# A two-part network on one core: first norms summed on TensorE, rotary tables moved, the FFN's scale deferred

## The chip, the cores and the metric

The kernel runs on one core of a Trainium2 chip. The metric is the device time of one execution in microseconds: the median of 3 runs is 1226.24 us (1225.2 to 1228.88). The profiled execution took 1224.34 us, with a span of 1222.2 us between its first and last instruction.

## The reference

Everything is fp32, for 256 positions of 1024 channels. The first block has two layers of a pooling mixer with dilated attention, a squared-ReLU FFN, and a gated per-layer embedding. The second block is one layer with modulated norms, a gated delta rule in both directions over a context and the latent, a short convolution, a Fourier branch, gates over the three, and a SwiGLU.

```
hn = rmsnorm(h, norm1[i]);  z = hn @ w_in[i]          # u, q, k, v;  q, k get rotary on 16 of 64 dims
h = h + concat([pool(u), attention(q, k, v)]) @ w_out[i]
hn = rmsnorm(h, norm2[i])
h = h + square(relu(hn @ w_up[i])) @ w_down[i]
h = h + sigmoid(rmsnorm(h, norm3[i]) @ w_gate[i]) * (p[i] @ w_ple[i])
...
mod = silu(c) @ w_mod + b_mod;  h = modulate(x, norm1_g, sh1, sc1);  hc = modulate(ctx, ...)
o_ctx, o_lat = bidir_gated_delta(context, latent)      # chunks of 64, a triangular inverse per chunk
x = x + g1 * (gates_0 * y_dn + gates_1 * y_sc + gates_2 * y_fn) @ w_o
x = x + g2 * swiglu(modulate(x, norm2_g, sh2, sc2))
return rmsnorm(x, final_g)
```

A row's scale commutes with both the ReLU (it is positive) and the matrix product over channels: with a row factor r, `square(relu(r·y)) @ w = r² · (square(relu(y)) @ w)`.

## The kernel before

Activations lie feature by position: `h` is 128 partitions by 8 blocks of 256 positions. Weights come in units of 512 KB by DMA into `wst` (three buffers, issued on SyncE's queue). ScalarE rounds a half of a unit to its high part `wh` (L262), VectorE takes the remainder `wl` (L263), and each product is three matmuls, hi·hi, lo·hi and hi·lo (`mm3`, L274). Operands are split the same way into `xh` and `xl` (L297, L298; L911, L912 for modulated norms). PSUM has four `acc` and four `bank` tiles. A norm's gain goes into the split; its row factor is applied to the product. For that `sumsq` squares `h` by two blocks (L309), adds the squares as `ssp` (L317, L319, L323), `col_sums` adds over partitions by a matmul with ones, `root` finds the inverse root by nine small operations on VectorE (`rsv`, `rsy`, `rst`, L345 to L361), and `across` turns it into a row (L370) where one is wanted.

`proj` does the first projection by four quarters of 256 channels; its norm's squares are added on GpSimd. `ffn` runs 16 steps of two `up` units and, one step behind, two `down` units into the four `acc`; the products of the first steps wait for the row of roots and are then scaled and rectified in one (L716). `residual` (L704) adds the accumulators to `h`. `gate` follows it directly.

Side work runs as generators: `beside(gen, rate)` attaches one, and `tick` in the matmul helpers advances it `rate` steps per unit. Such are the `modulation` (48 loads of `w_mod`, 512 KB each, and products with `c` on VectorE, L882; parts in three groups, beside the first FFN, later, and in the mixer), `context` (the context's half of the delta rule, between the layers' attention and beside the second FFN) and the recurrence in the mixer. There the triangular inverses are built by blocks: GpSimd and three DMAs (`there`, `back`, `xc`, L1275 to L1301) make the base blocks, and `dn_merge` joins them on TensorE (`U,al`; `U` and `Tm` on VectorE, L1317). `self.trip` says after how many steps the joining follows the round trip. `dn_scan` makes four steps for the latent: `S,kT`, then VectorE's `dr` (L1374, L1375), `dr,W`, `dv`, `S,qg`. A scheduler lists each engine's instructions in one order; at run time each engine works its list front to back. `np1` and `np2` count halves of weights whose `wl` goes to GpSimd.

Of the kernel before, what the change touches and what calls it, by code (L numbers as in the profile page):

```python
# [230 lines left out]
class Net:  # L231
# [218 lines left out]
    def rotary(self):  # L450
# [42 lines left out]
    def proj(self, i, b, x, r):  # L493

        nc = self.nc
        z = self.b1.tile([P, 2, 512], F32, name="zv" if b > 2 else "zqk")
# [4 lines left out]
        first = r is None
        if first:
            if i == 0:
                self.setup2()
            r = self.norm_cols(self.h)
        for t in range(2):
            nc.scalar.activation(z[:, t], pt[t], AF.Copy, scale=r[:, t:t + 1])
        return (z, r) if first else z

    def rotate(self, z):  # L510
        nc = self.nc
        zz = z.rearrange("p t (h d) -> p t h d", d=HD)
        x1, x2 = zz[:, :, :, 0:8], zz[:, :, :, 8:16]
        co = self.cos[:, :, None, :].to_broadcast([P, 2, 8, 8])
        si = self.sin[:, :, None, :].to_broadcast([P, 2, 8, 8])
        w = [self.b1.tile([P, 2, 8, 8], F32, name=f"rot{j}", bufs=1) for j in range(4)]
# [182 lines left out]
    def residual(self, acc):  # L699
        h = self.h  # L700
        for j in range(4):
            for n in ((0, 1), (1, 2)) if j == 3 else ((0, 2),):
                js = slice(2 * j + n[0], 2 * j + n[1])
                self.nc.vector.tensor_add(h[:, js], h[:, js], acc[j][:, n[0]:n[1]])  # L704

    def ffn(self, i):
# [17 lines left out]
        r = []  # L724
        steps = self.row_steps_sb(self.h, r)
        next(steps)
        wait = []
        for f in range(16):
            bv = self.bank2()
            if f == 0 and self.ko & 4:  # L730
                self.cols_into(bv, [self.a["w_up"][i, n] for n in range(2)], x, True)
            for n in range(2):
                if f or not self.ko & 4:
                    self.cols_into(bv[:, n:n + 1], [self.a["w_up"][i, 2 * f + n]], x)
                if f == self.at[0] and n == self.at[1]:
                    next(steps)
                if f == self.at[2] and n == self.at[3]:
                    run(steps)
                    for b in wait:
                        square(b)  # L740
                    wait = None
            if wait is not None:
                wait.append(bv)
            else:
                square(bv)
                while len(pend) > 1:
                    down(False)
        self.residual(down(True))
# [171 lines left out]
    def context(self, d, e):  # L920
# [17 lines left out]
        yield from self.modulate(Halves(hc), self.gains[:, 1], self.mod[:, 0, 1], x)  # L938
# [836 lines left out]
    def run(self):  # L1775
# [5 lines left out]
        self.np1 = 3  # L1781
        self.np2 = 3
# [17 lines left out]
        self.rp = 0  # L1800
# [13 lines left out]
        self.trip = 10  # L1814
        self.mod_parts = (((1, 0, 2), (3,), (4, 5)), ((1, 0, 2), (), (3, 4, 5)), ((1, 0, 2, 3), (), (4, 5)), ((1, 0), (), (2, 3, 4, 5)))[1]
# [47 lines left out]
```

## Time and profile before

| | |
|---|---|
| median of 3 runs | 1226.24 us (1225.2 to 1228.88) |
| profiled execution, span | 1224.34 us, 1222.2 us |
| granted TensorE clock, mean | 0.986 |
| TensorE (PE) busy | 1174.3 us (96%) |
| VectorE (DVE) busy | 899.3 us (74%) |
| ScalarE (ACT) busy | 635.6 us (52%) |
| GpSimd (POOL) busy | 119.9 us (10%) |
| DMA | 221.43 MB, 181 GB/s |

In the rows below, "idle 5.35 <-DVE U L1317" in square brackets is how long the engine stood before an instruction and what released it. A granted clock of 1.00 is 2.4 GHz throughout, 0.50 would be 1.2 GHz throughout. A row of several instructions (xN) gives the time from the first's start to the last's end. An fp32 matmul of few columns appears as two rows.

### The profile page before, as it was taken

How to read it: one execution, taken by the hardware profiler on the slowest of the kernel's cores; microseconds unless marked ns; L12 is line 12 of the kernel's file. 1: busy time of each engine (PE TensorE's matmuls, PEld its weight loads, DVE VectorE, ACT ScalarE, POOL GpSimd, SP SyncE). 2: the span in 40 equal slices, each digit the busy share in tenths (PEclk: the TensorE clock that was granted, in tenths of full speed). 3: DMA queues.
4: the chain of work that ended last, by engine and by line, in shares of the span. 5: the costliest groups of instructions: out<-in, count | busy, mean ns of one | idle time of the engine just before them, and what ended most of it. 6: DMA issues, size and time to landing. Idle time of an engine off the chain costs nothing.

```text
span 1222.2 us, 24807 instructions
## 1 busy us (share of the span) xinstructions
PE 1174.3 (96%) x9882; PEld 1111.4 (91%) x9882; DVE 899.3 (74%) x1804; ACT 635.6 (52%) x1250; POOL 119.9 (10%) x207
## 2 busy tenths in 40 slices
PE   8999899999999989999999999997999999999997
PEld 6779899999977889999999979897989998999996
DVE  6998997556998488675657899897655768555555
ACT  5654645545755565644445555544333546544444
POOL 1000000000010000064000130275000000000000
PEclk9999999999999999999999989999999998999998
DMA  6767688555553645556444525677422452655552
GB/s 223 238 199 249 208 297 278 189 194 190 164 174 121 200 139 164 182 165 207 156 147 164 171 91 164 226 270 243 142 89 100 173 195 99 213 185 189 186 180 84
DMA packets 65779, 221.43 MB, mean 181 GB/s; under 512 B 10048, under 2 KB 11456, under 8 KB 65664
## 3 DMA queue, kind: packets, MB, share of 16 engines
q1 hardware_dynamic: 64800, 218.29, 53.4%
q0 software_dynamic: 864, 1.57, 0.6%
q8 instruction: 77, 1.26, 0.4%
q14 instruction: 38, 0.31, 0.1%
HBM read 218.00 MB, written 1.84 MB: 180 GB/s over the span
## 4 chain that ended last, share of the span: by engine, by line
PE 72%; DVE 13%; DMA 6%; POOL 4%; issue 3%; ACT 2%; SPq 0%; DVEq 0%; POOLq 0%; ACTq 0%
PE acc L274 38%; PE bank L274 33%; DVE wl L263 4%; DMA wmst<-w_mod 2%; DVE xl L298 1%; POOL bo L1288 1%; POOL bz L1289 1%; ACT wh L262 1%; DVE wmst L882 1%; PE bank L565 1%; DVE h L704 1%; DVE cy L1044 1%; DMA back<-bzt 1%; DVE qkT L533 1%; DMA pt<-pT 0%
## 5 line engine op out<-in xcount | busy, mean ns | idle before, releaser
L262 ACT ACTIVATE wh<-wst 128x512 fp32r<-128x512 f32 x708 | 411.9, 624 | 427.4 <-PE bank L274 157.3
L263 DVE TENSOR_TENSOR wl<-wst,wh 128x512 fp32r<-128x512 f32 x702 | 470.1, 703 | 208.5 <-ACT wh L262 208.0
L274 PE MATMUL bank<-xl,wh 128*128 128x256 f32 x992 | 280.5, 283 | 2.1 <-DVE xl L298 2.1
L274 PE MATMUL bank<-xh,wl 128*128 128x256 f32 x992 | 279.4, 282 | 2.9 <-DVE wl L263 2.9
L274 PE MATMUL bank<-xh,wh 128*128 128x256 f32 x992 | 281.3, 284 | 0.8 <-ACT wh L262 0.8
L274 PE MATMUL acc<-al,wh 128*128 128x256 f32 x688 | 191.6, 279 | 0.0
L274 PE MATMUL acc<-ah,wl 128*128 128x256 f32 x688 | 191.3, 279 | 0.0
L274 PE MATMUL acc<-ah,wh 128*128 128x256 f32 x688 | 191.2, 279 | 0.0
L274 PEld LDWEIGHTS bank<-xh,wl 128*128 128x128 f32 x992 | 187.0, 189 | 4.3 <-DVE wl L263 4.3
L274 PEld LDWEIGHTS bank<-xl,wh 128*128 128x128 f32 x992 | 187.0, 189 | 2.8 <-DVE xl L298 2.7
L274 PEld LDWEIGHTS bank<-xh,wh 128*128 128x128 f32 x992 | 187.1, 189 | 1.6 <-ACT wh L262 1.2
L274 PE MATMUL acc<-xh,wh 128*128 128x256 f32 x640 | 183.4, 287 | 2.2 <-ACT xh L911 2.2
L274 PE MATMUL acc<-xl,wh 128*128 128x256 f32 x640 | 182.0, 285 | 1.5 <-DVE xl L912 1.5
L274 PE MATMUL acc<-xh,wl 128*128 128x256 f32 x640 | 181.1, 284 | 0.5 <-DVE wl L263 0.4
L274 PEld LDWEIGHTS acc<-al,wh 128*128 128x128 f32 x688 | 129.0, 188 | 0.0
L274 PEld LDWEIGHTS acc<-ah,wl 128*128 128x128 f32 x688 | 128.9, 188 | 0.1
L274 PEld LDWEIGHTS acc<-ah,wh 128*128 128x128 f32 x688 | 128.9, 188 | 0.0
L274 PEld LDWEIGHTS acc<-xh,wh 128*128 128x128 f32 x640 | 121.6, 190 | 4.7 <-ACT xh L911 2.8
L274 PEld LDWEIGHTS acc<-xl,wh 128*128 128x128 f32 x640 | 121.5, 190 | 2.9 <-DVE xl L912 1.7
L274 PEld LDWEIGHTS acc<-xh,wl 128*128 128x128 f32 x640 | 121.9, 191 | 1.5 <-DVE wl L263 0.9
L274 PE MATMUL acc<-wl,xh 128*128 128x512 f32 x176 | 70.6, 401 | 2.5 <-DVE wl L263 2.4
L274 PE MATMUL acc<-wh,xh 128*128 128x512 f32 x176 | 70.8, 406 | 1.1 <-ACT wh L262 1.1
(365 smaller groups left out, 1564.8 us busy)
## 6 DMA issues: line engine op xcount, KB each, us to landing
wst<-w_up SPq DMA_DIRECT2D x64, 512.0 KB, 4.2
wst<-w_down SPq DMA_DIRECT2D x64, 512.0 KB, 4.2
wmst<-w_mod SPq DMA_DIRECT2D x48, 512.0 KB, 4.8
wst<-w_fin SPq DMA_DIRECT2D x44, 512.0 KB, 3.2
wst<-w_in SPq DMA_DIRECT2D x39, 512.0 KB, 3.6
wst<-w_mgate SPq DMA_DIRECT2D x24, 512.0 KB, 3.3
wst<-w_fout SPq DMA_DIRECT2D x22, 512.0 KB, 3.2
wst<-w_qkv SPq DMA_DIRECT2D x20, 512.0 KB, 3.4
```

Source lines behind the costliest of these rows:

```text
L262: nc.scalar.activation(wh[:, c:c + n], st[:, c:c + n], AF.Copy)
L263: i = (nc.gpsimd if self.onpool > 0 else nc.vector).tensor_tensor(wl[:, c:c + n], st[:, c:c + n], wh[:, c:c + n].bitcast(F32), op=OP.subtract)
L274: self.nc.tensor.matmul(out, lhsT, rhs, start=start, stop=stop, skip_group_check=skip)
L298: nc.vector.scalar_tensor_tensor(xl[:, k], src, gain, xh[:, k].bitcast(F32), op0=OP.mult, op1=OP.subtract)
L533: nc.vector.tensor_copy(qk[:, :, t * P:(t + 1) * P], bk.rearrange("p (c q) -> p c q", c=4))
L565: nc.tensor.transpose(bk[:, c * P:(c + 1) * P], s[:, g, c * P:(c + 1) * P], self.ident)
L704: self.nc.vector.tensor_add(h[:, js], h[:, js], acc[j][:, n[0]:n[1]])
L882: nc.vector.scalar_tensor_tensor(pr, st, 1.0, cv[v], op0=OP.mult, op1=OP.mult, accum_out=mod[:, part, v, k:k + 1])
L1044: nc.vector.scalar_tensor_tensor(y4[:, j], pad[:, j, :, tap:tap + CHUNK], w[:, j, tap:tap + 1], y4[:, j], op0=OP.mult, op1=OP.add)
L1288: pool.tensor_tensor(o, lt[:, c:, j:c].to_broadcast([P, n, c]), Z[:, j:c, 0:c].to_broadcast([P, n, c]), op=OP.mult)
L1289: pool.tensor_tensor(Z[:, c:, 0:c], Z[:, c:, 0:c], o, op=OP.subtract)
```

## The change

1. The first norm of each layer is summed by quarters. Behind each quarter of the first projection, two blocks of `h` are squared on ScalarE and summed over partitions by four matmuls with ones into one bank. `norm_cols` and GpSimd's adds go.
2. The rotary tables (`rp` 0 to 1) and their two loads are made behind the second projection, not in `setup`. They are expanded to all heads, and a rotation takes three operations on 128x256 in place of twelve on 128x64.
3. The FFN no longer waits for its row of roots: ReLU on ScalarE, squares as before, and `residual` multiplies each accumulator by the row of 1 / mean square (`mean_square_steps`, no root) before adding it.
4. `mod_parts` puts 32 of the 48 `w_mod` units beside the first FFN (24 before), 16 later, none in the mixer (24 before); the first rate is 0.55 for 0.85.
5. `np1`, `np2`: six halves of `wl` go from GpSimd to VectorE. `trip` 10 becomes 13, and the context's norm gives way four times more.

```
-            r = self.norm_cols(self.h)
+            if first:
+                sq = self.t2k("sq")
+                nc.scalar.activation(sq, self.h[:, 2 * q:2 * q + 2], AF.Square)
+                for n in range(2):
+                    for t in range(2):
+                        self.mm(cs[:, t:t + 1], sq[:, n, t * P:(t + 1) * P], self.ones[:, 0:1], q == 0 and n == 0 and t == 0,
+                                q == 3 and n == 1, True)
...
+            r = self.rsqrt(cs, 2, D)
...
-        for o, x, c in zip(w, (x1, x2, x2, x1), (co, si, co, si)):
-            for t in range(2):
-                nc.vector.tensor_mul(o[:, t], x[:, t], c[:, t])
-        for t in range(2):
-            nc.vector.tensor_sub(x1[:, t], w[0][:, t], w[1][:, t])
-            nc.vector.tensor_add(x2[:, t], w[2][:, t], w[3][:, t])
+        nc.vector.tensor_mul(co, zz, self.cos)
+        nc.vector.tensor_mul(si, zz[:, :, ::-1], self.sin)
+        nc.vector.tensor_add(zz, co, si)
...
-                self.nc.vector.tensor_add(h[:, js], h[:, js], acc[j][:, n[0]:n[1]])
+                a = acc[j][:, n[0]:n[1]]
+                if row is not None:
+                    t = self.t2k("fft")[:, n[0]:n[1]]
+                    self.nc.vector.tensor_mul(t, a, row[:, None, :].to_broadcast([P, n[1] - n[0], T]))
+                    a = t
+                self.nc.vector.tensor_add(h[:, js], h[:, js], a)
+
+    def mean_square_steps(self, h, res):
+        ss = self.sumsq(h)
+        yield
+        v = self.sm.tile([P, 2], F32, name="rsv2")
+        nc.vector.tensor_scalar(v, self.col_sums((ss,)), 1.0 / D, EPS, op0=OP.mult, op1=OP.add)
+        nc.vector.reciprocal(v, v)
+        yield
+        r = self.sm.tile([P, T], F32, name="nrow")
+        nc.scalar.activation(r, self.across(v)[:, 0:T], AF.Copy)
+        res.append(r)
...
-                nc.vector.scalar_tensor_tensor(t[:, n], bv[:, n], 0.0, r[0], op0=OP.max, op1=OP.mult)
+            if f in (1, 3, 5):
+                next(steps, None)
+            nc.scalar.activation(t, bv, AF.Relu)
...
-        self.residual(down(True))
+        self.residual(down(True), r[0])
...
-            self.beside(self.modulation(*self.mod_parts[0]), 0.85)
+            self.beside(self.modulation(*self.mod_parts[0]), 0.55)
...
+        for _ in range(4):
+            yield
...
-        self.np1 = 3
-        self.np2 = 3
+        self.np1 = 0
+        self.np2 = 0
...
-        self.trip = 10
+        self.trip = 13
```

Three places of the lists, as the scheduler orders them. First VectorE at the end of the first FFN, where `acc` holds the `down` products and `xl` is the gate's operand; before:

```order
L263 TENSOR_TENSOR wl<-wst,wh 128x512 x4
L704 TENSOR_TENSOR h<-h,acc 128x512 x2
L298 SCALAR_TENSOR_TENSOR xl<-h,k_norm_242,xh 128x256 x2
L704 TENSOR_TENSOR h<-h,acc 128x512
L298 SCALAR_TENSOR_TENSOR xl<-h,k_norm_242,xh 128x256 x2
L704 TENSOR_TENSOR h<-h,acc 128x256 x2
L298 SCALAR_TENSOR_TENSOR xl<-h,k_norm_242,xh 128x256 x4
L317 TENSOR_TENSOR ssp<-sq 128x512
```

and in the changed kernel:

```order
L263 TENSOR_TENSOR wl<-wst,wh 128x512 x4
L715 TENSOR_TENSOR fft<-acc,nrow 128x512
L717 TENSOR_TENSOR h<-h,fft 128x512
L715 TENSOR_TENSOR fft<-acc,nrow 128x512
L298 SCALAR_TENSOR_TENSOR xl<-h,k_norm_242,xh 128x256
L717 TENSOR_TENSOR h<-h,fft 128x512
L715 TENSOR_TENSOR fft<-acc,nrow 128x512
L298 SCALAR_TENSOR_TENSOR xl<-h,k_norm_242,xh 128x256
L717 TENSOR_TENSOR h<-h,fft 128x512
L715 TENSOR_TENSOR fft<-acc,nrow 128x256 x2
L717 TENSOR_TENSOR h<-h,fft 128x256 x2
L298 SCALAR_TENSOR_TENSOR xl<-h,k_norm_242,xh 128x256 x6
```

Five multiplications (L715) stand between the accumulators and the additions, and six of the eight `xl` come behind the last of them.

Second, VectorE at the start of the second FFN, behind the attention's residual (`ssp` and `ss` are the sums of squares of the context's norm and of the FFN's, `rsv` begins the root); before:

```order
L298 SCALAR_TENSOR_TENSOR xl<-h,k_norm_240,xh 128x256 x4
L317 TENSOR_TENSOR ssp<-sq 128x512
L263 TENSOR_TENSOR wl<-wst,wh 128x512
L319 TENSOR_TENSOR ssp<-ssp,sq 128x512
L263 TENSOR_TENSOR wl<-wst,wh 128x512
L319 TENSOR_TENSOR ssp<-ssp,sq 128x512
L317 TENSOR_TENSOR ssp<-sq 128x512
L323 TENSOR_TENSOR ss<-ssp 128x256
L263 TENSOR_TENSOR wl<-wst,wh 128x512
L345 TENSOR_SCALAR rsv_5261<-bank 128x2
```

and in the changed kernel:

```order
L298 SCALAR_TENSOR_TENSOR xl<-h,k_norm_240,xh 128x256 x4
L263 TENSOR_TENSOR wl<-wst,wh 128x512 x7
L756 TENSOR_TENSOR al<-fft,ah 128x512
L263 TENSOR_TENSOR wl<-wst,wh 128x512
L317 TENSOR_TENSOR ssp<-sq 128x512
L263 TENSOR_TENSOR wl<-wst,wh 128x512
L319 TENSOR_TENSOR ssp<-ssp,sq 128x512 x2
L263 TENSOR_TENSOR wl<-wst,wh 128x512
L323 TENSOR_TENSOR ss<-ssp 128x256
```

The sums move behind eight `wl` and the first product `al`, and of the two norms only one is left there.

Third, TensorE in the latent's scan (`S` the state, `W` and `dr` the step's operands; the other matmuls are those of the branches); before, in a step with 19 other matmuls up to `dr,W`, its last rows:

```order
L274 MATMUL acc<-xl,wh 128x256
L274 MATMUL acc<-xh,wl 128x256
L274 MATMUL acc<-xh,wh 128x256
L274 MATMUL bank<-dr,W 64x128 x8
L370 MATMUL bank<-k_c_ident,dex 128x128 x4
```

and in the changed kernel, the first step:

```order
L274 MATMUL acc<-xh,wl 128x256
L274 MATMUL bank<-S,kT 64x128 x8
L274 MATMUL bank<-dr,W 64x128 x8
L370 MATMUL bank<-k_c_ident,dex 128x128 x4
L274 MATMUL bank<-dv_11174,tokk 128x128 x3
L274 MATMUL acc<-S,qg 64x128 x8
L274 MATMUL acc<-dv_11176,att 64x128 x8
```

Nothing stands between `S,kT` and `dr,W` in the first and second step any more; the third and fourth keep their 19.

## Rows read from the trace of the kernel before

**Rows 1.** The page, part 1: busy us, share of the span, instructions.

```profile
PE 1174.3 (96%) x9882; PEld 1111.4 (91%) x9882; DVE 899.3 (74%) x1804; ACT 635.6 (52%) x1250; POOL 119.9 (10%) x207
```

**Rows 2.** Windows: from:to length, engines' busy us (instructions), PEclk, DMA share, GB/s

```profile
450.00:480.00 30.00, 29.82 (x239) 28.53 (x238) 23.93 (x65) 17.44 (x37) 0.81 (x6) 0.94 0.43 141
690.00:720.00 30.00, 24.91 (x181) 21.88 (x181) 26.94 (x63) 15.63 (x37) 16.81 (x30) 0.89 0.27 89
810.00:840.00 30.00, 29.55 (x251) 29.34 (x249) 29.97 (x55) 15.61 (x29) 24.34 (x36) 1.00 0.88 303
840.00:870.00 30.00, 24.26 (x327) 23.32 (x325) 21.25 (x47) 9.44 (x18) 3.97 (x6) 0.89 0.59 191
```

**Rows 3.** Waits of PE: engine, tile, awaited; us in total, times, longest.

```profile
PE bank L274 <- DVE U L1317: 5.4, 1, 5.4
...
PE bank L274 <- DVE rsy L358: 3.4, 1, 3.4
PE bank L370 <- DVE rsy L361: 3.1, 2, 1.9
PE bank L1143 <- DVE tokk L1134: 2.8, 1, 2.8
...
PE acc L274 <- ACT xh L911: 2.2, 2, 1.3
PE bank L274 <- DVE xl L298: 2.1, 3, 1.3
...
PE acc L274 <- DVE xl L912: 1.5, 1, 1.5
```

**Rows 4.** Timeline of DVE, start: start, us, engine, line, operation [idle before].

```profile
11.78 1.29 DVE L263 TENSOR_TENSOR wl<-wst,wh 128x512 fp32r<-128x512 f32 x2
...
14.20 2.04 DVE L263 TENSOR_TENSOR wl<-wst,wh 128x512 fp32r<-128x512 f32 x2 [0.34 <-ACT wh L262]
```

**Rows 5.** Timeline of PE, start.

```profile
12.52 0.51 PE L274 MATMUL acc<-wl,xh 128*128 128x512 f32 x1 [1.13 <-DVE wl L263]
```

**Rows 6.** Groups by line and form: busy us, mean ns, idle before.

```profile
L716 DVE SCALAR_TENSOR_TENSOR fft<-bank,nrow 128x256 f32<-128x256 f32 x64 | 24.4, 419 | 21.7 <-PE bank L274 21.4 <-ACT nrow L404 0.2
...
L263 POOL TENSOR_TENSOR wl<-wst,wh 128x512 fp32r<-128x512 f32 x6 | 10.6, 1772 | 130.3 <-ACT wh L262 130.3
...
L704 DVE TENSOR_TENSOR h<-h,acc 128x512 f32<-128x512 f32 x12 | 8.2, 684 | 1.0 <-PE acc L274 1.0
...
L519 DVE TENSOR_TENSOR rot<-zqk,rcos 128x64 f32<-128x64 f32 x24 | 5.3, 221 | 0.9 <-ACT zqk L507 0.8
...
L274 PE MATMUL bank<-ones,ss 128*128 128x1 f32 x36 | 5.2, 248 | 4.9 <-DVE rsy L358 3.4 <-DVE ss L1654 1.5
...
L704 DVE TENSOR_TENSOR h<-h,acc 128x256 f32<-128x256 f32 x8 | 3.0, 417 | 0.0
```

**Rows 7.** Timeline of DVE, start of the first FFN.

```profile
119.50 1.22 DVE L882 SCALAR_TENSOR_TENSOR wmpr<-wmst,cv 128x1024 f32<-128x1024 f32 x1 [0.86 <-DMA wmst<-w_mod]
```

**Rows 8.** Timeline of DVE, start of the second FFN.

```profile
452.39 0.16 DVE L361 SCALAR_TENSOR_TENSOR rsy<-rst,rsy 128x2 f32<-128x2 f32 x1
```

**Rows 9.** Timeline of PE, end of the first FFN.

```profile
310.97 0.38 PE L274 MATMUL bank<-xh,wl 128*128 128x256 f32 x1 [0.46 <-DVE wl L263]
```

**Rows 10.** Timeline of DVE, start of the mixer.

```profile
694.76 1.23 DVE L360 TENSOR_TENSOR rst<-rst,lv 128x4 f32<-128x4 f32 x1
...
700.55 2.76 DVE L996 SCALAR_TENSOR_TENSOR mt<-h,lgg,lrows 128x128 f32<-128x128 f32 x4
```

**Rows 11.** Timeline of DVE, the round trip of the latent.

```profile
851.71 0.76 DVE L1317 TENSOR_TENSOR Tm<-xc,k_d_blk 128x256 f32<-128x256 f32 x2 [6.55 <-DMA xc<-back]
```

**Rows 12.** Timeline of PE, the second scan step.

```profile
906.69 1.09 PE L274 MATMUL bank<-S,kT 128*64 128x128 f32 x16
...
910.15 1.09 PE L274 MATMUL bank<-dr,W 64*64 64x128 f32 x16
```

**Rows 13.** Timeline of DVE, the second scan step.

```profile
909.15 0.69 DVE L1375 TENSOR_TENSOR dr<-tokv,dr 128x512 f32<-128x512 f32 x1
```

More of the change, by code (lines that the diff above doesn't have):

```diff
@@ L479, in rotary @@
         nc.scalar.activation(self.cos, t, AF.Sin)
+        full = [self.b1.tile([P, 16, 2, 8], F32, name=n, bufs=1) for n in ("fcos", "fsin")]
+        for i in range(2):
+            for x in range(2):
+                for o, src, f in zip(full, (self.cos, self.sin), (1.0, 2.0 * x - 1.0)):
+                    nc.vector.tensor_scalar(o[:, 8 * i:8 * i + 8, x], src[:, i][:, None, :].to_broadcast([P, 8, 8]), f, None,
+                                            op0=OP.mult)
+        self.cos, self.sin = full
     def tokens_into(self, pt, x, q, w):
@@ L497, in proj @@
         pt = [self.acc.tile([P, 512], F32, name="acc") for _ in range(2)]
+        first = r is None
+        if first:
+            cs = self.bank()[:, 0:2]
         for q in range(4):
@@ L500, in proj @@
             self.tokens_into(pt, x, q, w)
-        first = r is None
+            if first:
+                sq = self.t2k("sq")
[4 more added lines that the diff above has]
+                                q == 3 and n == 1, True)
         if first:
@@ L511, in rotate @@
         nc = self.nc
[L512 to L516, printed above, removed]
-        for o, x, c in zip(w, (x1, x2, x2, x1), (co, si, co, si)):
-            for t in range(2):
-                nc.vector.tensor_mul(o[:, t], x[:, t], c[:, t])
-        for t in range(2):
-            nc.vector.tensor_sub(x1[:, t], w[0][:, t], w[1][:, t])
-            nc.vector.tensor_add(x2[:, t], w[2][:, t], w[3][:, t])
+        zz = z.rearrange("p t (h d) -> p (t h) d", d=HD)[:, :, 0:16].rearrange("p n (x j) -> p n x j", x=2)
+        co, si = (self.b1.tile([P, 16, 2, 8], F32, name=f"rot{j}", bufs=1) for j in range(2))
+        nc.vector.tensor_mul(co, zz, self.cos)
+        nc.vector.tensor_mul(si, zz[:, :, ::-1], self.sin)
+        nc.vector.tensor_add(zz, co, si)
     def scores(self, i, b, z, S):
@@ L697, in downward, with residual @@
         return down
-    def residual(self, acc):
+    def residual(self, acc, row=None):
         h = self.h
@@ L711, in ffn @@
         down = self.downward(self.a["w_down"][i], 32, pend)
-        def square(bv):
+        r = []
+        steps = self.mean_square_steps(self.h, r)
+        for f in range(16):
+            bv = self.bank2()
+            if f == 0 and self.ko & 4:
+                self.cols_into(bv, [self.a["w_up"][i, n] for n in range(2)], x, True)
+            else:
+                for n in range(2):
+                    self.cols_into(bv[:, n:n + 1], [self.a["w_up"][i, 2 * f + n]], x)
+            if f in (1, 3, 5):
+                next(steps, None)
             t = self.sm.tile([P, 2, T], F32, name="fft", tag="w2k", bufs=self.nw2k)
-            for n in range(2):
-                nc.vector.scalar_tensor_tensor(t[:, n], bv[:, n], 0.0, r[0], op0=OP.max, op1=OP.mult)
             ah = self.sm.tile([P, 2, T], F32R, name="ah", tag="w2k", bufs=self.nw2k)
             al = self.sm.tile([P, 2, T], F32R, name="al", tag="w2k", bufs=self.nw2k)
+            nc.scalar.activation(t, bv, AF.Relu)
             nc.scalar.activation(ah, t, AF.Square)
@@ L722, in square @@
             pend.append((ah, al))
[L724 to L747, printed above, removed]
-        self.residual(down(True))
+            if f:
+                down(False)
+        self.residual(down(True), r[0])
     def ple(self, i):
@@ L937, in context @@
         x = self.xc = []
-        yield from self.modulate(Halves(hc), self.gains[:, 1], self.mod[:, 0, 1], x)
+        norm = self.modulate(Halves(hc), self.gains[:, 1], self.mod[:, 0, 1], x)
+        next(norm)
+        for _ in range(4):
+            yield
+        yield from norm
         yield
@@ L1799, in run @@
         self.po = 0
-        self.rp = 0
+        self.rp = 1
         self.sparts = 0
@@ L1813, in run @@
         self.mod_rate = 0.8
[L1814 to L1815 removed]
+        self.trip = 13
+        self.mod_parts = ((1, 0, 2, 3), (4, 5), ())
         with ExitStack() as ctx:
```

3 lines of the change are left out of this document (1 added, 2 removed).

## The prediction

> **What bounds the kernel now.** I read the busy times first, then the table of 30 us windows, then the waits of TensorE, and last the timeline of each stretch that stood out. TensorE (PE) is busy for 1174.3 of 1222.2 us [rows 1]; VectorE (DVE) and the DMAs matter only where PE waits for them, so an edit is worth what it does to one of PE's waits. The waits come to about 48 us (1222.2 − 1174.3), in few places: one of 5.4 us for `U`, one of 3.4 for `rsy` at L358, 2.8 for `tokk`, 2.1 for three `xl`, 2.2 and 1.5 for `xh` and `xl` of the modulated norm [rows 3]. Behind the larger ones the granted clock is below one: 0.94 in 450 to 480, 0.89 in 690 to 720 and in 840 to 870 [rows 2]. A mean of 0.89 over 30 us loses (1 − 0.89) × 30 = 3.3 us, one of 0.94 loses 1.8. So a long wait is paid for twice, with its idle time and with a stretch behind it at 1.2 GHz.
>
> Durations are from the profiled execution, 1224.34 us with a span of 1222.2. It lies 1.9 us under the median of the three timed runs, 1226.24. I sum differences against the profiled one and take them from the median at the end. Each term has my value, then its two ends; plus is time gained.
>
> **The change, part by part.**
>
> *A, start: +1.9 (0 to 3.5).* The rotary angles leave DVE's first 12 us, and the first norm's adds leave GpSimd. PE waits 1.13 us there for a `wl` [rows 5]; two `wl` take 2.04 beside GpSimd's adds and 1.29 without them [rows 4], 0.75 less. 1.13 + 0.75 = 1.9. The low end is a start that the weight loads pace anyway; the high end adds a second wait as long as the first.
>
> *B, column sums on PE: −5.1 (−8 to −3).* Each layer issues 16 matmuls by 1 column where it had 2; in fp32 each is two rows of the trace, so 32 rows for 4. One such row costs 5.2 / 36 = 0.144 us with the ends of the groups [rows 6], so 28 × 0.144 = 4.0 per layer at most. Rows issued back to back should cost less: I take 3.5 in layer 1, where PE has no wait to fill, and 1.6 in layer 0, where part falls into the waits of A.
>
> *C, rotary: −0.3 (−3 to +1.7).* A rotation's 12 operations of 0.22 us [rows 6] become 3 on 128x256, 0.417 each by the nearest form [rows 6]: 2.65 to 1.25, six times. The tables (built for 16 heads, with 8 more small operations) move behind the second projection; their 4 to 5 us (8 more operations at 0.22 and the angles' small ones) about cancel the first three rotations, and layer 1's rotations give some 0.7 back. Their two small loads move with them on SyncE's queue, behind weights that are prefetched.
>
> *D, start of the first FFN: +3 (1 to 4.5).* Three `xl` waits, 2.1 us [rows 3], follow a DVE queue in which a `w_mod` product waited 0.86 us for its load and ran 1.22, between the residual adds [rows 7]. The norm's sums leave the queue ahead of the first `wl`, and the row of inverse roots, 1.2 of the 3.1 us waited for `rsy` at L361 [rows 3], is no longer awaited by any FFN product. A `w_mod` product stays between the adds, so I count 3 of these 3.3 us.
>
> *E, ends of both FFNs: −5.9 (−8.3 to −2).* The scale by the row now stands at the residual: five multiplications more, 3 × 0.684 + 2 × 0.417 = 2.9 us on DVE at the adds' durations [rows 6], in the one chain that leads from the last `down` matmul to the gate's `xl`. PE already waits at its end, 0.46 us for a `wl` queued behind it [rows 9], so nothing hides them but the first, which runs while later accumulators finish: 2.9 − 0.7 = 2.2, twice. In layer 1 the context's last merge (four 128x512 operations, 2.7 us) now also stands ahead of the gate's later `wl`: −1.5.
>
> *F, start of the second FFN: +5.2 (3.4 to 6).* Before, the sums and roots of two norms (context and FFN) alternate on DVE with `wl` until 452.4 [rows 8], and PE stands at the context's column sum: 3.4 us [rows 3], and 1.8 of clock behind it [rows 2]. After, the FFN's sums come eight `wl` later and its root has two operations instead of nine (no cover is needed: PE has `up` and `down` matmuls queued).
>
> *G, start of the mixer: +4 (−3 to +7).* Six halves of weights come from GpSimd to DVE. GpSimd takes 1.772 us for one [rows 6], DVE 0.65 (1.29 for two [rows 4]), so DVE gets 3.9 us more. Against that, DVE crawls beside GpSimd's: an operation on 4 columns, of a chain whose members take 0.16 elsewhere [rows 8], takes 1.23 (L360), and four `mt` of 128x128 take 2.76 [rows 10]. PE waits 2.2 + 1.5 for `xh` and `xl` there [rows 3] and loses 3.3 to the clock [rows 2]: 7 in all is the high end. If DVE's slow rows have another cause, 3.9 more work ahead of the first `mt` makes it −3. I take +4. The Trainium skill ("GPSIMD Engine Reference", Key points) says that GpSimd shares its SBUF interfaces with VectorE, with contention where a VectorE instruction has two SBUF inputs or a two-port mode. By that rule the holds are GpSimd's and leave with the six halves; by the durations alone the move would cost time. The slow rows bear the rule out.
>
> *H, keys: +0.5 (−1 to +2).* PE waits 2.8 for `tokk` [rows 3], behind a `w_mod` product of 1.22 [rows 7] that leaves; but its transposes now stand 15 matmuls earlier.
>
> *I, the wait for `U`: +7.3 (5.5 to 8.5).* DVE idles 6.55 us until a DMA brings `xc` back [rows 11]; PE idles 5.4, then runs at half clock. The merge is joined three yields later: `U,al` stands some 90 matmul rows further back in PE's stream, at 29.55 / 251 = 0.12 us a row [rows 2] over 10 us, and the 24 `w_mod` loads and their products leave the stretch 715 to 860, so the round trip shortens. 5.4 + most of 3.3 [rows 2].
>
> *J, the scan of the latent: −5.2 (−8 to 0).* By the order, two of four scan steps now have `dr,W` directly behind `S,kT`, where each step had 11 or 19 other matmuls. In between lie a product, a `wl` and the subtraction on DVE, which ends at 909.15 + 0.69 = 909.84 [rows 13], while `S,kT` ends at 906.69 + 1.09 = 907.78 [rows 12]: 2.1 us bare, and 0.5 for `dv` behind the transposes. 2 × 2.6. PE then started `dr,W` at 910.15 with no wait [rows 12]. The low end adds clock.
>
> *K, DVE time that comes free: +1 (0 to 2).* 64 products (L716, 24.4 us [rows 6]) become ReLUs on ScalarE, and 24 `w_mod` products go from the mixer to the FFNs, 8 and 16. In both FFNs PE is the bound, so little of this shows. The moved loads stand on SyncE's queue among the FFN's weights; a load that must wait for its buffer would hold weights, which I price in the low end of the range only.
>
> Sum: 1.9 − 5.1 − 0.3 + 3 − 5.9 + 5.2 + 4 + 0.5 + 7.3 − 5.2 + 1 = 6.4 us. 1226.2 − 6.4 = 1219.8 us (1217.9 for the profiled execution). All low ends together are −21.4, all high ones +30.2; the terms are mostly independent, so the range takes under half of that spread.
>
> **The rivals.**
>
> *Larger gain, 1207.* G, H and I at their high ends, with their half-clock stretches, and no bunching in the scan, as DVE has 24 × 1.22 = 29 us less before it [rows 7]: 6.4 + 3 + 1.5 + 1.2 = 12.1, and 5.2 + 2 without J and with a faster start: about 19. For it: the losses at J come from the static order alone. Against it: DVE keeps the `dr` chain, and nothing fills PE's queue between. Chance 0.2.
>
> *No change, 1226.* The gains of G aren't there (−3, as worked out above) and the round trip of `xc` still ends late (U gives 4, not 7.3): 6.4 − 7 − 3.3 = −3.9, less what lies between: −4 to +2. For it: the chain of GpSimd work and DMAs to `xc` is untouched. Against it: `U,al` stands 10 us later and the wait was 5.4. Chance 0.2.
>
> *Slower, 1232.* The new short waits bring the clock down. There are five (two FFN ends, two scan steps, the gate of layer 1): 2 × 2.9 + 2 × 2.6 + 2.7 = 13.7 us idle, and behind each a stretch at 1.2 GHz, priced at 1.8 as behind the wait of 3.4 [rows 2]: 9. That is 22.7 against the 11.1 of E and J: 6.4 − 11.6 = −5.2, 1231.4. It decides the sign once E and J together cost over 17.5. The Trainium skill ("TensorE: Matmul & The Clock Gate", Part 1) says that a monitor of PE's recent activity sets the clock, with the throttled state as the default; the windows with the waits of 3.4 and 5.4 us bear it out, and none here shows what a wait of 2 does alone. Chance 0.14.
>
> **How the numbers follow.** The forecast case, 1213 to 1224, has the rest, 0.46. A measurement of this kernel tells 0.3% from no change, 3.7 us. Faster than 1222.5 takes the larger gain (0.2) and most of the forecast case (0.42), with 0.03 of the no-change case: 0.65. Within 1222.5 to 1229.9: 0.17 of no change, 0.04 of the forecast and 0.01 of the slower case: 0.22. Slower: 0.13. The range of 8 in 10 runs from the middle of the larger gain to the near edge of the slower case: 1209 to 1230.
>
> **What would show it.** Right: no wait for `U` and clock 1.0 in its window; no wait for `rsy` at the second FFN; `wl` on DVE alone; DVE well under its 29.97 of 30 us in 810 to 840 [rows 2]. For the losses: waits on `dr` and `dv` in the scan of some 2 and 0.5 us, a wait for `xl` of some 2 at both gates. Wrong: E or J absent (the gain is then nearer to 17), the wait for `U` still over 2, a clock below 1 at the gates or in the scan, or waits for `wst` loads in the FFNs.

## The result, and the profile after

The changed kernel takes 1219.7 us, the median of 10 runs (1217.82 to 1223.45); the kernel before takes 1226.23 in 10 runs beside it (1221.83 to 1229.24). The ratio is 0.995, with a 95% interval of 0.9934 to 0.9966: 6.5 us faster by the medians. The forecast was 1219.8. The total came out as forecast, but not every term that makes it up, as the stages and the experiments show.

The profiled execution took 1221.31 us, 1.6 above its median, and the one of before lay 1.9 below its own. So the two traces differ by 2.7 us where the medians differ by 6.5, and a stage of one trace is a rough measure: the first FFN, whose instructions are the same in five traces (the changed kernel, e1, e2, e7, e8), takes 183.6 to 187.3 us in them.

The page of the changed kernel, part 1: TensorE is busy 7 us longer (before in [rows 1]), VectorE 30 us and GpSimd 30 us shorter.

```profile
PE 1181.2 (97%) x9938; PEld 1119.4 (92%) x9938; DVE 869.4 (71%) x1696; ACT 650.1 (53%) x1282; POOL 89.8 (7%) x193
```

The longest waits of TensorE after, columns as in [rows 3]:

```profile
PE bank L274 <- DVE dr L1391: 4.5, 2, 2.3
PE bank L274 <- DVE wl L263: 4.0, 5, 1.8
PE bank L1129 <- DVE kT L1100: 2.8, 1, 2.8
PE bank L274 <- DVE xl L298: 2.1, 2, 1.7
PE bank L370 <- DVE rsy L361: 1.9, 1, 1.9
...
PE acc L274 <- ACT xh L923: 1.5, 2, 1.2
```

The waits for `U`, for `rsy` at L358 and nearly all of that for `tokk` (a key operand of the context) are gone. New are two waits on `dr` in the scan, one on `kT` (the keys) in the context, and a longer one on a `wl`. The 1.9 left on `rsy` at L361 is the norm at the very end, which both kernels have.

Windows of the changed kernel, columns as in [rows 2]:

```profile
300.00:330.00 30.00, 28.27 (x227) 27.86 (x226) 27.08 (x60) 18.93 (x38) 0.00 (x0) 0.94 0.47 152
450.00:480.00 30.00, 29.97 (x255) 29.26 (x255) 25.75 (x56) 21.15 (x43) 0.00 (x0) 1.00 0.59 189
510.00:540.00 30.00, 26.52 (x202) 25.41 (x201) 26.68 (x56) 16.04 (x43) 6.01 (x12) 0.94 0.81 280
690.00:720.00 30.00, 27.73 (x202) 25.67 (x203) 22.08 (x64) 18.41 (x41) 7.14 (x24) 0.89 0.30 94
810.00:840.00 30.00, 30.00 (x254) 30.00 (x253) 20.18 (x32) 16.29 (x30) 19.49 (x41) 1.00 0.73 218
840.00:870.00 30.00, 30.00 (x367) 28.79 (x367) 18.90 (x37) 13.55 (x26) 0.00 (x0) 1.00 0.50 170
900.00:930.00 30.00, 27.29 (x281) 24.54 (x280) 17.09 (x30) 7.69 (x14) 0.00 (x0) 1.00 0.21 73
```

Three of these windows in the kernel before:

```profile
300.00:330.00 30.00, 29.54 (x250) 29.21 (x249) 27.43 (x61) 20.30 (x42) 0.00 (x0) 1.00 0.51 171
510.00:540.00 30.00, 29.34 (x262) 28.36 (x262) 21.35 (x32) 14.90 (x27) 14.75 (x18) 1.00 0.48 150
900.00:930.00 30.00, 30.00 (x304) 26.62 (x304) 20.29 (x37) 10.82 (x23) 0.00 (x0) 1.00 0.21 72
```

Against these and [rows 2]: TensorE is full and its clock 1.00 in 450 to 480 and 840 to 870, where it was 0.94 and 0.89. 690 to 720 reads 0.89 again, though not in every profile of the same code (e11 below). New low spots are 300 to 330 (the first gate) and 510 to 540 (the context beside the second FFN), each 0.94, and the scan, 27.29 of 30 in 900 to 930. VectorE falls from 29.97 to 20.18 in 810 to 840.

A table of stages, from the start of the instruction named in the traces (us); `zqk` is the product of the first projection, scaled by its norm. Columns 3 and 4 belong to the experiments e5 and e9 below; "second FFN and gate" runs from the attention's residual to the gate's first addition.

| stage (from, to) | before | after | e5 | e9 |
|---|---|---|---|---|
| start to first `zqk` | 26.18 | 28.14 | 27.76 | 23.69 |
| rest of layer 0's attention | 91.78 | 91.44 | 92.04 | 92.74 |
| first FFN | 185.62 | 183.97 | 181.60 | 182.56 |
| first gate | 19.26 | 21.32 | 20.83 | 21.35 |
| layer 1, to its first `zqk` | 23.96 | 26.21 | 26.20 | 23.95 |
| rest of layer 1's attention | 88.08 | 89.42 | 89.42 | 87.96 |
| second FFN and gate | 241.28 | 240.78 | 238.26 | 238.20 |
| mixer, to the last `h<-h,bg` | 280.94 | 273.69 | 267.61 | 268.23 |

Three places of the trace after carry the new waits. The first gate, behind the five multiplications; then the second FFN, where TensorE waits for a `wl` and for the keys of the context:

```profile
309.29 0.39 PE L274 MATMUL bank<-xl,wh 128*128 128x256 f32 x1 [1.71 <-DVE xl L298]
```

```profile
502.16 0.39 PE L274 MATMUL bank<-xh,wl 128*128 128x256 f32 x1 [1.84 <-DVE wl L263]
...
520.91 0.44 PE L1129 MATMUL bank<-k_c_ident,kT 128*128 128x128 f32 x2 [2.84 <-DVE kT L1100]
```

Between these two ScalarE stands for a weight load, in the window where the DMAs are at 0.81:

```profile
514.32 0.63 ACT L262 ACTIVATE wh<-wst 128x512 fp32r<-128x512 f32 x1 [1.80 <-DMA wst<-w_down]
```

And the scan, the first two steps:

```profile
898.71 1.09 PE L274 MATMUL bank<-dr,W 64*64 64x128 f32 x16 [2.16 <-DVE dr L1391]
...
900.59 0.71 PE L274 MATMUL bank<-dv,tokk 64*128 64x128 f32 x6 [0.21 <-DVE dv L1401]
...
916.44 1.09 PE L274 MATMUL bank<-dr,W 64*64 64x128 f32 x16 [2.30 <-DVE dr L1391]
...
918.31 0.71 PE L274 MATMUL bank<-dv,tokk 64*128 64x128 f32 x6 [0.20 <-DVE dv L1401]
```

### The profile page after: what moved, and what is told of

Its sections match the earlier page's. It is cut to its first block, busy times and chain, and to the rows that moved or that the text cites. A ratio compares the mean times of both kernels' runs of the same rounds, so it can differ in the third digit from the quotient of the medians.

```text
span 1219.5 us, 24817 instructions
## 1 busy us (share of the span) xinstructions
PE 1181.2 (97%) x9938; PEld 1119.4 (92%) x9938; DVE 869.4 (71%) x1696; ACT 650.1 (53%) x1282; POOL 89.8 (7%) x193
## 3 DMA queue, kind: packets, MB, share of 16 engines
HBM read 218.00 MB, written 1.84 MB: 180 GB/s over the span
## 4 chain that ended last, share of the span: by engine, by line
PE 62%; DVE 13%; issue 12%; DMA 8%; POOL 3%; ACT 2%; SPq 0%; DVEq 0%; POOLq 0%; ACTq 0%
PE acc L274 36%; PE bank L274 24%; DMA wmst<-w_mod 5%; DVE wl L263 4%; DVE wmst L894 1%; DVE cy L1060 1%; PE bank L572 1%; POOL bz L1305 1%; ACT wh L262 1%; POOL bo L1304 1%; DVE qkT L540 0%; DVE wmpr L894 0%; DVE S L551 0%; DMA wst<-w_out 0%; DMA wst<-w_down 0%
```

## The experiments

Each was timed beside the kernel before; ratios are to it, with their 95% intervals. The open question was not whether the kernel is faster but which edits made it so. Theory A was the prediction's sum: each edit worth what its own term says. The rival B was that one edit, the moved `w_mod` loads, does the work of several and that others only cost.

**e1, the joining at ten steps again.**

```
-        self.trip = 13
+        self.trip = 10
```

> The changed kernel with the joining back at ten steps (trip 10), all else as changed. Theory A (the terms I and J of the prediction are both true as sized): the scan's bunching goes (order: 12, 20, 20 and 27 rows between S,kT and dr,W), worth 4.5 us by the two waits on dr in the trace after, and the wait for U comes back as 5 to 7 us of idle and clock: 1219.7 - 5 + 7.3 = 1222, 0.9965 of before; U waited for 4 us or more. Rival B (the w_mod loads and products made the round trip late, not the early joining): U waited for under 2 us, the scan's waits gone: 1219.7 - 5 + 1 = 1215.5, 0.991 of before.

1216.38 us (6 runs), 0.991 (0.989 to 0.993): B. The scan's waits are gone, and there is no wait for `U`, though `U,al` stands where it stood before in TensorE's stream. VectorE's first operation on `xc`, for which it waited 6.55 us in [rows 11]:

```profile
842.02 0.76 DVE L1333 TENSOR_TENSOR Tm<-xc,k_d_blk 128x256 f32<-128x256 f32 x2 [1.14 <-DMA xc<-back]
```

The round trip is shorter at the same start. GpSimd's base blocks before, first and last operation of the chain of small products, and then the issue of `xc`:

```profile
815.23 0.54 POOL L1288 TENSOR_TENSOR bo<-blt,bz 128x15 f32<-128x15 f32 x1
...
837.56 1.04 POOL L1291 COPY bzt<-bz 128x256 f32<-128x256 f32 x1
...
846.29 3.28 POOL L1301 DMA_DIRECT2D xc<-back  x4 [5.60 <-DMA back<-bzt]
```

and in e1:

```profile
814.02 0.22 POOL L1304 TENSOR_TENSOR bo<-blt,bz 128x15 f32<-128x15 f32 x1
...
829.14 0.96 POOL L1307 COPY bzt<-bz 128x256 f32<-128x256 f32 x1
...
833.98 1.67 POOL L1317 DMA_DIRECT2D xc<-back  x2 [1.79 <-DMA back<-bzt]
```

From the first `bo` to `bzt` it was 837.56 − 815.23 = 22.3 us and is 829.14 − 814.02 = 15.1; the wait for `back` was 5.60 and is 1.79. Nothing of that chain was edited. What left its stretch are the `w_mod` products on VectorE and their loads. The other traces agree: with `w_mod` units there (before, e4, e11) the chain takes 21.8 to 22.4 us, without them 14.4 to 15.2 in all ten others. It is the products more than the loads. One of them in the kernel before, and the GpSimd operation that started beside it:

```profile
819.59 1.21 DVE L882 SCALAR_TENSOR_TENSOR wmst<-wmst,cv 128x1024 f32<-128x1024 f32 x1
```

```profile
819.72 1.21 POOL L1288 TENSOR_TENSOR bo<-blt,bz 128x48 f32<-128x48 f32 x1
```

and the same operation in e1:

```profile
816.61 0.27 POOL L1304 TENSOR_TENSOR bo<-blt,bz 128x48 f32<-128x48 f32 x1
```

GpSimd's ends 0.13 us after VectorE's. Six of the 30 operations lie mostly beside a `w_mod` product in that way and take 1.13 us on the mean; the 20 of the same stretch with little or none of one beside them take 0.54, with the loads running all the while. In e1 the four that find VectorE idle take 0.28. The Trainium skill ("GPSIMD Engine Reference", Key points) says that GpSimd shares its SBUF interfaces with VectorE and that VectorE's instructions with two SBUF inputs contend for them. The `w_mod` products have two such inputs, and the 7.2 us agree, in the other direction than term G: VectorE's work slows GpSimd's.

**e2, the joining at twelve.**

```
-        self.trip = 13
+        self.trip = 12
```

> The changed kernel with trip 12. By the order, 4, 22, 20 and 27 rows lie between S,kT and dr,W (none in two steps at 13), and U,al stands 25 to 70 rows further back than at 10. Theory A: U is waited for under 1.5 us and the waits on dr are one of 2 instead of two of 2.3: 1217, 0.9925. Rival B: no wait for U either, 1216.5, about the same as trip 10. If the scan's bunching is worth nothing (the time comes back elsewhere): 1219.7, 0.995.

1219.38 us (6 runs), 0.9943 (0.9923 to 0.9963). No wait for `U` and none on `dr`, yet no gain over thirteen: the mixer is 4.2 us shorter than in the changed kernel, and the second FFN with its gate 2.4 longer, with a wait of 3.29 us for the gate's `ss`, which stands behind the context's merge on VectorE. One constant sets both joinings. The expectation missed that: its third number came out, but not for the reason given with it.

**e3, the FFN's scale as before.**

```
-            nc.scalar.activation(t, bv, AF.Relu)
+                nc.vector.scalar_tensor_tensor(t[:, n], bv[:, n], 0.0, r[0], op0=OP.max, op1=OP.mult)
...
-        self.residual(down(True), r[0])
+        self.residual(down(True))
```

> The changed kernel with the FFN's scale as before: products wait for the row of roots, are scaled and rectified in one on VectorE, the residual only adds. Theory A (terms D, E, F): the 1.7 us wait and the half clock at the first gate go (2 to 2.5 us gained), in layer 1 nothing shows at the gate; waits for rsy of 1.2 at the first FFN and 2 or more at the second come back, with clock: 1219.7 - 2.3 + 1.2 + 3.5 = 1222, 0.9965. Rival: the multiplications at the residual cost more than the late row did: 1217, 0.9925.

1221.86 us (12 runs), 0.9972 (0.9952 to 0.9991): theory A's number, though it is only 2.2 us above the changed kernel and the two intervals overlap. By stages the first FFN is 185.85, which lies within the 183.6 to 187.3 of the changed code, and the first gate 19.21, 2.1 shorter: in layer 0 no gain of the deferred scale is shown. In layer 1 the two stages take 241.77, 1.0 longer. The wait of 1.2 us for `rsy` at the first FFN came back. The one of 3.4 at the second did not: the context's norm gives way in this kernel too. In its place TensorE waits 1.80 us for a `wh`, and the clock is 0.94 in 450 to 480. So that the deferred scale ends the wait of 3.4 is not shown; the later context's norm may do it alone.

**e4, the w_mod units as before.**

```
-            self.beside(self.modulation(*self.mod_parts[0]), 0.55)
+            self.beside(self.modulation(*self.mod_parts[0]), 0.85)
...
-        self.mod_parts = ((1, 0, 2, 3), (4, 5), ())
+        self.mod_parts = ((1, 0, 2), (), (3, 4, 5))
```

> The changed kernel with the w_mod units as before: 24 beside the first FFN at 0.85, 24 in the mixer. Theory A: VectorE gets 24 x 1.22 = 29 us back in the mixer, PE waits there for tokk again (2.8) and runs slower, about 5 us lost; the two waits at the context in the second FFN (1.8 and 2.8 us in the trace after) go: 1219.7 + 5 - 4 = 1221, 0.996. Rival (the w_mod products in the second FFN cost as much as they save in the mixer, or more): 1217 to 1219.5. Rival (freed DMA and VectorE time in the mixer is the main source of the gain): 1226, 1.0.

1220.18 us (6 runs), 0.9945 (0.9928 to 0.9962): the same as the changed kernel, between theory A and the first rival. Its second FFN runs 212.59 us from residual to residual, 6.2 less than the changed kernel's 218.77, and its mixer 280.92, 7.2 more than 273.69. Windows of e4, for the context's keys and for the scan:

```profile
510.00:540.00 30.00, 29.07 (x258) 27.75 (x257) 19.10 (x39) 18.53 (x47) 2.67 (x8) 1.00 0.44 150
900.00:930.00 30.00, 27.60 (x263) 24.95 (x257) 17.36 (x30) 7.08 (x13) 0.00 (x0) 0.94 0.21 71
```

The context has VectorE at 19.10 of 30 and the DMAs at 0.44, where the changed kernel has 26.68 and 0.81; its wait for `wl` is gone and that for `kT` shrinks to 0.30. `U` is waited for 0.38 and 0.19 us only: joining later does remove nearly all of that wait too, but the scan's two waits on `dr` (2.15 and 2.29) are the price. The kernel before took 1226.35 beside this one: without the move of the loads the other edits gain 6.2 us, so the strong form of rival B is out.

**e10, the kernel before with the w_mod units moved**, the fourth corner of that square.

```
-            self.beside(self.modulation(*self.mod_parts[0]), 0.85)
+            self.beside(self.modulation(*self.mod_parts[0]), 0.55)
...
+        self.mod_parts = ((1, 0, 2, 3), (4, 5), ())
```

> The kernel before with one edit, the placing of the w_mod units as in the changed kernel (32 beside the first FFN at 0.55, 16 beside the second, none in the mixer). Theory A (the move takes out of the mixer about what it puts into the FFNs): no wait for U (5.4 before), no wait for tokk behind a w_mod product, the mixer 8 to 10 us shorter, both FFNs together 6 to 8 us longer, with waits of 1.5 to 3 us at the context's keys in the second: 1223 to 1226, 0.998 to 1.0. Rival (the move alone makes the changed kernel's gain): 1219, 0.994. The wait for U still over 3 us would speak for the joining as its cause.

1221.61 us (12 runs), 0.9969 (0.9954 to 0.9984), a little better than theory A and well short of the rival. At ten steps the wait for `U` is gone. VectorE's first `Tm`:

```profile
846.92 0.76 DVE L1317 TENSOR_TENSOR Tm<-xc,k_d_blk 128x256 f32<-128x256 f32 x2 [3.30 <-DMA xc<-back]
```

The mixer takes 272.43, 8.5 less than before (7.1 less than in the second profile of it, e11); the first FFN takes 187.89, 2.3 more, and the second 223.57, 1.9 more. The four corners by the medians: the move alone gains 4.0 us (1225.65 beside it), the other edits alone 6.2 (e4), both together 6.5. The gains do not add up, since each side ends the same wait.

**e7, both first norms on GpSimd again.**

```
-                        self.mm(cs[:, t:t + 1], sq[:, n, t * P:(t + 1) * P], self.ones[:, 0:1], ...)
...
-            r = self.rsqrt(cs, 2, D)
+            r = self.norm_cols(self.h)
```

> The changed kernel with the first norms of both layers summed on GpSimd as before, everything else as changed. Theory A (term B: 28 more rows of PE per layer cost 3.5 us in layer 1 and part of that in layer 0, and the removed adds gave less): 1219.7 - 3.5 = 1216 to 1217.5, 0.992 to 0.993; the first projection of layer 1 starts its scores 2 us earlier. Rival (GpSimd's adds hold VectorE as much as the ones cost PE): 1219 to 1221, 0.9945, with two wl of 2 us and PE waiting at 12 and 19 us again.

1217.54 us (6 runs), 0.9932 (0.9907 to 0.9957), theory A. Its first `zqk`, and the changed kernel's:

```profile
23.80 0.69 ACT L514 ACTIVATE zqk<-acc,rsy 128x512 f32<-128x512 f32 x1 [1.87 <-DVE rsy L361]
```

```profile
28.14 0.69 ACT L519 ACTIVATE zqk<-acc,rsy 128x512 f32<-128x512 f32 x1 [3.32 <-DVE rsy L361]
```

4.3 us earlier; in layer 1 the stage takes 23.96 for 26.21 and the rest of the attention 88.12 for 89.42, 3.6 less in all. By the medians e7 gains 2.2 us; its profiled run, 1213.41, lies 4.1 below its median. The rows that cost this, in the changed kernel's start:

```profile
7.15 1.70 PE L274 MATMUL bank<-ones,sq 128*128 128x1 f32 x8
...
13.12 1.20 PE L274 MATMUL bank<-ones,sq 128*128 128x1 f32 x8
...
19.82 0.95 PE L274 MATMUL bank<-ones,sq 128*128 128x1 f32 x8
...
23.46 0.95 PE L274 MATMUL bank<-ones,sq 128*128 128x1 f32 x8
```

Together 1.70 + 1.20 + 0.95 + 0.95 = 4.8 us for 32 rows; the first eight take 212 ns each, the last 119. What differs is TensorE's pace. Two matmuls of one form, around the second group of rows:

```profile
10.14 0.63 PE L274 MATMUL acc<-wl,xh 128*128 128x512 f32 x1
...
14.74 0.40 PE L274 MATMUL acc<-wl,xh 128*128 128x512 f32 x1
```

The first start 0.43 us apart, the later ones 0.23: about half the pace, as at 1.2 GHz. A window over the start reads 1.00 even so, because the trace has no clock entry before 13.65 us and what is missing counts as full. In e6, where the matmuls run at full pace from the first, the same first eight rows take 125 ns each:

```profile
6.93 1.00 PE L274 MATMUL bank<-ones,sq 128*128 128x1 f32 x8
```

GpSimd's adds slow VectorE in e7 as they did before (two `wl` take 2.07 us, two `xl` 2.42), but TensorE hardly waits for it: the first projection has waits of 0.89, 0.50 and 0.48 us, without the rotary angles.

**e8, six halves of weights on GpSimd again.**

```
-        self.np2 = 0
+        self.np2 = 3
```

> The changed kernel with np2 back at 3: six halves of weights on GpSimd at the mixer's start. Theory A (term G: the operations that GpSimd's halves hold on VectorE cost more than 3.9 us): slow rows again (an rst of 1.2, four mt of 2.3 to 2.8), waits for xh and xl of 3 us and more, 2 to 4 us slower: 1222 to 1224, 0.997. Rival B (VectorE's slow rows come from elsewhere or are covered, now that it has no w_mod products): same or up to 2 faster, 1217.5 to 1220.

1227.98 us (12 runs, 1221.51 to 1236.3), 1.0024 (1.0 to 1.0048), worse than theory A said. The start of the mixer, from the gate's first addition to the first matmul with `wbh`, takes 34.63 us for 30.08; over all traces it takes 31.0 to 34.9 with the halves on GpSimd (four traces) and 26.0 to 31.8 without (nine). VectorE there, in e8 and then in the changed kernel:

```profile
705.89 2.73 DVE L1012 SCALAR_TENSOR_TENSOR mt<-h,lgg,lrows 128x128 f32<-128x128 f32 x4
...
709.46 1.27 DVE L924 SCALAR_TENSOR_TENSOR xl<-mt,mod,xh 128x256 fp32r<-128x256 f32 x2
```

```profile
708.80 1.95 DVE L1012 SCALAR_TENSOR_TENSOR mt<-h,lgg,lrows 128x128 f32<-128x128 f32 x4
...
711.14 1.27 DVE L924 SCALAR_TENSOR_TENSOR xl<-mt,mod,xh 128x256 fp32r<-128x256 f32 x2
```

Four `mt` take 2.73 beside GpSimd's halves and 1.95 without them. The two `xl` read 1.27 in both, so not every slow row is due to the halves; GpSimd still has its own products on `x` there. TensorE waits 1.9 and 1.5 us for `xh` and `xl`, as expected; the slow `rst` of 1.2 did not come back (0.16).

**e11, the kernel before once more**, no edit.

> The kernel before once more, for a second profile of its start. If the start's time is set by the code, the first zqk comes at 26.2 us again within 0.5; if by the phase of TensorE's clock, as the changed kernel's seven profiles suggest (26.2 to 29.9), it may lie 2 us off.

The first `zqk` came at 26.22 (26.18 in the first profile, 25.97 in e10): the start of the kernel before is set by its code, though its matmuls reach full pace at 10 us in two of these profiles and run at it from the first in e10. The start of the changed kernel is not. Of it there are eight profiles with the same code: 24.95 in e6, 26.22 in e2, 27.75 to 28.33 in five, 29.93 in e3. They lie in the order in which the 128x512 matmuls reach full pace: at once in e6, at once but with a stretch at half pace from 8.3 to 11.7 us in e2, by 12.7 to 14.4 in the five, at 17.6 in e3. So the phase that the expectation asks about matters, and only where the column sums are on TensorE. The second profile also reads a clock of 1.00 at the start of the mixer, with TensorE no busier than in [rows 2]:

```profile
690.00:720.00 30.00, 23.21 (x182) 20.14 (x183) 26.80 (x63) 16.12 (x38) 16.76 (x30) 1.00 0.30 97
```

**e5, the w_mod units where there is room.** Trip 10; 24 units beside the first FFN, 16 with the latent's scan, 8 beside the SwiGLU; each product of the last 24 is ordered behind the newest `wl`.

```
+            yield from weave(self.dn_scan(dl, el, st, oT), self.modulation(*(3, 4)))
...
+            if f == 1:
+                self.beside(self.modulation(*(5,)), 0.3)
...
+        self.trip = 10
+        self.mod_parts = ((1, 0, 2), (), ())
```

> Trip 10, and the w_mod units put where VectorE and the DMAs have room: 24 beside the first FFN (rate 0.85), 16 woven with the latent's scan and held behind the newest wl in VectorE's order, 8 beside the SwiGLU. Theory A (24 products beside the second FFN and 8 beside the first cost 6.2 and 1.4 us, by the stages of e4 against the changed kernel): from trip 10's 1216.4 to 1209 to 1211, 0.986 of before; the second FFN takes 213 to 216 us from the attention's residual to its own, not 219 to 222. Rival B (the products and their 12 MB cost the same wherever they stand): 1216, 0.991, with new waits in the scan or the SwiGLU.

1210.01 us (5 runs), 0.9876 (0.9852 to 0.9899): theory A, and no rival's number. The second FFN takes 216.98 us, a little over the 213 to 216 that were expected; the mixer takes 267.61, 6.1 less than the changed kernel's and 3.3 more than e1's.

**e6, the embedding's product as cover for the residual.** The operands are split before the last `down`, the matmuls run behind the residual.

```
-        self.residual(down(True), r[0])
+        ple = self.ple(i)
+        next(ple)
+        self.residual(down(True), r[0])
+        run(ple)
```

> As e5_late_mod, and the embedding's product (48 matmuls of 256 columns, 5.7 us) moved from before the FFN to between its last down matmul and the gate, its operands split before. Theory A (the five multiplications at the residual cost what PE waits for at the gate, 1.7 us and a stretch of half clock, in both layers): no wait for xl at either gate, 2 to 2.5 us gained twice against e5: 1205.5, 0.983. Rival (the work is only moved: its wl and pl lengthen the chain on VectorE): same as e5 within 1.5 us, with the wait for xl still there.

1218.75 us (6 runs), 0.9946 (0.9926 to 0.9966), 8.7 us slower than e5; neither theory. TensorE's waits at the first gate:

```profile
305.17 0.38 PE L274 MATMUL bank<-xh,wh 128*128 128x256 f32 x1 [0.65 <-ACT xh L297]
307.21 0.39 PE L274 MATMUL bank<-xl,wh 128*128 128x256 f32 x1 [1.66 <-DVE xl L298]
...
311.52 0.39 PE L274 MATMUL bank<-xh,wl 128*128 128x256 f32 x1 [2.00 <-DVE wl L263]
```

The one wait became three, 4.3 us in all, and VectorE stood 5.73 us before the residual for a `wh`. From the pooling to the gate e6 takes 236.84 and 268.37 us in the two layers, e5 232.78 and 266.34: 4.1 and 2.0 lost. The next projection lost 2.7 more (28.89 for 26.20) and the mixer 4.7 (272.33 for 267.61), for reasons that I did not find.

**e9, e5 with the norms on GpSimd** (the edit of e7).

> As e5_late_mod (trip 10, late w_mod), with both first norms summed on GpSimd as before. Theory A (term B is a loss in both layers, 4.2 us in layer 0 and 2.3 in layer 1 by the stages of e7; the start depends on the clock phase by some 1.8): from 1210 to 1204 to 1207, 0.983. Rival (e7's start was a lucky phase, and only layer 1's 2.3 is real): 1207.5 to 1209, 0.986.

1203.98 us (4 runs), 0.9819 (0.9799 to 0.9838), theory A at its lower end, 6.0 us under e5. It is the fastest, 21.7 us under the kernel before and 15.7 under the changed one.

## Why the prediction was right, and which terms were not

The forecast of a gain of 6.4 us met one of 6.5. That they agree to 0.1 us is luck: the interval of the ratio alone leaves 4 to 8 us, and the terms have errors of both signs that cancel. By the medians of the experiments, undoing one edit costs 8.3 us for the six halves of weights (e8), 2.2 for the scale (e3, the intervals overlap) and 0.5 for the moved loads (e4), and it gains 2.2 for the column sums (e7) and 3.3 for the joining (e1). The rotary tables and the context's norm were not taken alone.

- A, start: said +1.9. The first `zqk` comes 26.18 − 23.80 = 2.4 us earlier when the norms stay on GpSimd (e7; 2.5 in e9). The size is right, and the rotary angles alone bring it: GpSimd's adds are back in e7 and so is a pair of `wl` of 2.07, so the 0.75 that A took from that pair is not borne out.
- B, column sums: said −5.1, 3.5 in layer 1 and 1.6 in layer 0. Layer 1 is right: 3.6 from the gate's addition to the attention's residual (115.63 in the changed kernel, 112.08 in e7). Layer 0 was mis-sized: −4.3 (e7) and −4.1 (e9 against e5) to the first `zqk`. The step that failed is "part falls into the waits of A": A removes most of those waits, and the start runs at half pace for longer. Where the matmuls run at full pace from the first, the loss is 24.95 − 23.69 = 1.3 (e6 against e9). Whether the early rows themselves delay the full pace is not shown; in the five profiles without them it came by 10.4 us, in six of the eight with them later.
- C, rotary: said −0.3. The rest of layer 1's attention is 1.3 longer in the changed kernel, but in e7 and e9, with the new tables and the old sums, it takes 88.12 and 87.96 as before: that loss is B's. Layer 0's is 0.3 shorter. No experiment takes the tables alone, so that they cost about nothing stays a reading of these traces.
- D, first FFN: said +3, and +1.65 in the traces of the stage table. With 32 `w_mod` units the same code reads 183.6 to 187.3 in five traces, against 185.6 and 185.7 in the two profiles of the kernel before, so no gain is shown there; with 24, as before, it reads 181.6 to 182.6 (e4, e5, e9), 3 to 4 less. The size was right for an FFN with 24; the eight units that moved in were priced at nothing, and take it back.
- E, residual: said −2.2 per layer and −1.5 for the merge. Layer 0: 21.32 − 19.26 = 2.1, with the wait of 1.71. Layer 1: no wait, because the context's merge (`U,al` and its partner, 2.1 us of TensorE each) now lies in the gate and fills it. What I had down as a further loss was the cover. With the merge back in the FFN (e1, e5) the wait of 1.7 appears there too.
- F, second FFN: said +5.2. FFN and gate together gain 0.5 in the stage table (to 240.78; 239.88 and 238.47 in e7 and e8 with the same code), but that stage also holds E's share in layer 1, −3.7, so 1.5 was to be seen there. In e5 it gains 3.0. The 3.4 us wait and its half clock went as said, but the step "so little of this shows" in K failed: the 16 `w_mod` units stand beside the context's keys, VectorE and the DMAs fill up, and waits of 1.84 and 2.84 us and a clock of 0.94 take their place. Moving them out is worth 3.9 to 6.2 (e4 against the three traces with the same code) or, with ten steps, 4.9 (e5 against e1, 216.98 for 221.83).
- G, mixer's start: said +4. The halves cost 4.5 there (e8), and 8.3 by the medians. The 3.3 us of clock in its high end came from a window that reads 1.00 in e11.
- H to K, rest of the mixer: G to K were to give 7.6, the mixer gave 7.25 (5.8 to 9.3 with the second profiles, e11 and e7). The sum holds and the attribution does not. Term I took the later joining and the shorter round trip as parts of one gain; either ends the wait, or nearly. e1 and e10 show that moving `w_mod` does it at ten steps, e4 that joining later leaves 0.6 us of it with the loads in place. With the loads moved the later joining then only costs: 2.16 + 0.21 + 2.30 + 0.20 = 4.9 us in the scan, where J said 5.2. Undoing it gives 3.3 us by the medians.

Of the rivals, the slower one did not come. It priced each new short wait at 1.8 us of clock. The wait of 1.7 at the first gate is in eight traces; in four of them the clock falls to 0.94 in 300 to 330 (the changed kernel, e1, e8, e9) and the gate takes 21.2 to 21.4 us, in the other four it stays at 1.00 (e2, e4, e5, e7) and the gate takes 20.8. So the fall comes or not behind the same wait, and costs 0.5. In the scan the clock stayed at 1.00 in the changed kernel and e7 and fell to 0.94 in e3, e4 and e8, with the same two waits. The larger gain had its causes right in part (the scan's bunching was avoidable), but it needed another kernel, e5 or e9.

## What to carry to other kernels

Work that is moved off a critical stretch has a price where it arrives: look at VectorE's and the DMAs' share in the windows of the destination before calling it free. Do not let two terms claim the same wait, one by removing it and one by hiding in it. When two edits attack one wait, run all four corners; here either ended it, their gains did not add up, and one of them was better undone. Before a stage is read to a microsecond, look at it in other traces of the same code.

## What was not expected of the hardware

A chain of 30 small GpSimd products took 22.3 us beside VectorE's `w_mod` products and 15.1 without them, so a transfer that such a chain feeds comes 7 us earlier with no edit to it; an operation of 0.27 us that starts beside a VectorE product of 1.21 took 1.21 itself. A sum over one column, two fp32 rows of TensorE's, costs 119 to 125 ns a row at full pace and 212 at the pace of the start, where the profile's windows read 1.00 although the matmuls take 0.63 us for 0.40. The clock is not a property of the code alone: in 690 to 720 it was 0.89 in the first profile of the kernel before and 1.00 in the second, and 0.89 in the changed kernel and 1.00 in e1.
